# The context between the two latent halves in a layer's value and gate projections

## The chip, the cores and the metric

The kernel runs on one core of a Trainium2 chip. Its time is device microseconds of one execution, as a median over runs. The engines are named as in the profile: PE is TensorE's matmul, PEld its weight load, DVE VectorE, ACT ScalarE, POOL GpSimd, SP SyncE, which issues most transfers.

## What is computed

A two-layer diffusion backbone over 1024 latent tokens (a grid of 16 rows of 64) with a prefix of 256 context tokens; the model is 1024 wide, all of it in float32. The first (even) layer is attention, global and windowed. The change lies in the second (odd) layer, which is the last, so only the latent tokens leave it:

```python
def odd_mixer(h_lat, h_ctx, w_in, w_out, dw_w, dw_b, ln_g, ln_b, rpb, update_ctx):
    cv, cgl, cg, dq, dk, dv, dg = split_cols(h_lat @ w_in, ODD_WIDTHS)
    x_cv, x_cgl, x_cg, x_dq, x_dk, x_dv, x_dg = split_cols(h_ctx @ w_in, ODD_WIDTHS)
    c_dk, c_dv = heads(x_dk, D_HEADS), heads(x_dv, D_HEADS)
    oc = conformer_conv(cv, cgl, cg, dw_w, dw_b, ln_g, ln_b)
    ...
    def d_row(args):
        ...
        kk = jnp.concatenate([c_dk, kr], axis=1)
        vv = jnp.concatenate([c_dv, vr], axis=1)
        return gqa_attend(qr[:, :, :, None, :], kk, vv, bias).reshape(bsz, GRID_W, D_W)
    ...
    y_lat = jnp.concatenate([oc, od * jax.nn.silu(dg)], axis=-1) @ w_out
```

Each of 8 heads of 64 attends from a grid row to the context and to the 8 grid rows around it, with a bias table. Keys and values are projected from latent and context tokens, queries and the gate dg from the latent tokens alone.

## The kernel before

**Precision.** A float32 product is made of three matmuls on a high and a low part of each operand (`mm3`, lines 320 to 322): hi x hi, hi x lo, lo x hi. A high part is a cast on ACT (L298), a low part a subtraction on POOL or DVE (L301). One projection of 128 output rows has a depth of 1024, eight blocks of 128, so 24 matmuls.

**Tokens.** They are kept transposed in three chunks: c = 0 is the context (256 columns), c = 1 and c = 2 are the latent halves (512 each); their high and low parts are called hc for the context and hh, hl for the halves. An accumulation fills one bank of PSUM, called p for these projections.

**Head pairs.** `d_proj(i)` projects pair i of heads (i = 0 to 3), in two parts. First come queries and keys with one set of weights. Then `load_w` brings the weights of value and gate (256 columns, eight blocks, from DRAM into wr, cast into wh on ACT and wl on POOL; there are eight places for wh and wl, so a block of the next set waits until the last projection that reads its place is through). Then a loop over the chunks in the order `VORD`, line 1207:

- the value projection of the chunk. For the context it is copied into vc (ACT, L1212); for a half the columns that its two windows need are copied into vT (ACT, L1217, two copies);
- for a half, the gate projection, its tanh on ACT (L1222) and two products on DVE into sgd (L1224), and the transfer GD to DRAM (L1225);
- transposes of the value in blocks of 128 (trv, PE, L1232): 2 for the context, 4 for half 1, 4 and 2 for half 2; their high and low parts into spv (ACT L298, DVE L301), and the transfer VD to DRAM (L1244).

The tiles sgd and vc, and later xs, a piece of the residual stream that ACT loads (L1411), share two buffers.

**Where the pairs run.** Pair 0 runs under the convolution (whose work is on DVE, POOL and ACT), pair 1 under the layer norm of its result, both with PE to themselves. Pairs 2 and 3 are woven between the steps of the second layer's attention. A group of that attention is one head and one half: it loads keys for a new head (KAt, L363), queries (QH, L1307 and L1308, three buffers; QL, L1309), values (Vt, L1334), bias tables (bm, L1311; bs, L1320) and the gate (gt, L1326) from DRAM, makes row maxima (mx, L1348 and L1356), scores (st, L467 and L471), and the sums over values (ov, L411 to L413), and stores y as O1d (L1379). The output projection (po, by `mm3` too) follows inside the same stretch; oc is the convolution's result as its operand.

**What sets the order.** The program is written as generators that are advanced in turns with fixed numbers (pumps for pairs 0 and 1, weights in a weave for pairs 2 and 3), and a scheduler then puts the instructions of each engine in an order by priority and expected readiness. Each engine works through its queue in that order. The order in `VORD` therefore shifts rows on all five engines.

Of the kernel before, what the change touches and what calls it, by code (L numbers as in the profile page):

```python
# [36 lines left out]
BSW, BMW = 1664, 1080  # L37
CWB = 12
VSH = 5
VORD = (1, 2, 0)  # L40
WBN = 8
TRV = "pp"
HALF = {'half': 3, 'hf': 2}
# [46 lines left out]
def tile_kernel(ctx: ExitStack, tc: tile.TileContext, a, out):  # L90
# [823 lines left out]
    def pair(name, n=512, tag="pair"):  # L914
        return (stg[0] if tag == "spo" else lp).tile([P, 2, NR * NW], F32R, tag=tag, name=nm(name), bufs=STG[tag])[:, :, :n]
# [189 lines left out]
    with ExitStack():  # L1105
# [67 lines left out]
        def d_proj(i):  # L1173
# [32 lines left out]
            vT = pair("vT", 640, "vT").bitcast(F32)  # L1206
            for c in VORD:
                t0, n = CHUNKS[c]
# [431 lines left out]
```

## Time and profile before

| | us |
|---|---|
| median of 3 runs | 1560.27 |
| lowest and highest | 1560.08, 1562.05 |
| profiled execution | 1561.07 |
| its span in the trace | 1559.3 |
| PE busy | 1453.3 (93% of the span) |
| mean granted clock of PE | 0.966 |

The span is the time from the first to the last record of the profiled execution; the rest of its time, 1.8 us, lies around it. A row of a timeline gives the start and the duration in us, engine, line, operation, output and inputs with their tiles, shape and count, and in brackets how long the engine was idle before it and what ended that. In the stage table each stretch has its length, then the busy time of each engine with the number of instructions, the granted clock of PE, the mean busy share of the 16 DMA engines, and GB/s. In the list of waits the numbers are the total, the times, and the longest. Busy time of PE is modelled from pipelined matmuls: a matmul of 512 columns lasts some 0.39 us, and the next starts 0.23 us after it.

### The profile page before, as it was taken

Reading aid. Unit: us, or ns where it says so; the run is one execution under the profiler, and the core shown is the slowest. Engines: PE = TensorE matmul, PEld = TensorE weight load, DVE = VectorE, ACT = ScalarE, POOL = GpSimd, SP = SyncE. Lnnn points to the kernel's source line nnn. Section 1 sums busy time; section 2 is a strip of 40 time slices with the busy share of each in tenths; the row PEclk is TensorE's granted clock in tenths of the full one; section 3 lists DMA queues with packets and bytes.
Section 4 is the critical chain, followed back from the end, with each engine's and each line's share of the span. In section 5 each row is a group of like instructions: output and inputs, shape, how many; then the busy total and the mean of one; then the engine's idle time right before and its main releaser. Section 6 shows DMA issues by size and latency. Waiting matters only on the chain.

```text
span 1559.3 us, 22034 instructions
## 1 busy us (share of the span) xinstructions
PE 1453.3 (93%) x6984; PEld 1174.9 (75%) x6984; DVE 1124.3 (72%) x2172; ACT 763.1 (49%) x1545; POOL 828.7 (53%) x762
## 2 busy tenths in 40 slices
PE   6989999998999999899999889999999998799995
PEld 1888977886888678588887668888787787687785
DVE  4898896788867677555478776999746456587676
ACT  2721354544453755555545655443333455555573
POOL 1561463555455776655646765664542333455575
PEclk9899999999999999999999999999999999899996
DMA  9548245423441135711111121213456888788722
GB/s 337 194 144 263 84 129 175 137 68 117 150 131 46 44 102 167 227 56 53 44 51 62 44 94 53 83 57 127 150 176 220 273 224 251 225 265 239 205 92 108
DMA packets 185613, 221.01 MB, mean 142 GB/s; under 512 B 17420, under 2 KB 139480, under 8 KB 185496
## 3 DMA queue, kind: packets, MB, share of 16 engines
q1 hardware_dynamic: 178832, 208.03, 43.3%
q10 hardware_dynamic: 6664, 11.57, 2.3%
q8 instruction: 55, 0.90, 0.2%
q14 instruction: 62, 0.51, 0.1%
HBM read 159.51 MB, written 60.03 MB: 141 GB/s over the span
## 4 chain that ended last, share of the span: by engine, by line
PE 66%; DVE 13%; DMA 10%; issue 4%; POOL 3%; ACT 2%; SPq 2%; ACTq 0%; DVEq 0%; POOLq 0%
PE p L322 6%; PE p L320 6%; PE p L321 6%; PE ov L411 4%; PE ov L413 4%; PE ov L412 4%; PE po L320 4%; PE po L321 4%; PE po L322 4%; PE st L471 3%; PE st L467 3%; DMA QH<-QD 3%; PE pq L322 2%; PE pq L321 2%; PE pq L320 2%
## 5 line engine op out<-in xcount | busy, mean ns | idle before, releaser
L301 POOL TENSOR_TENSOR pl<-pf,ph 128x512 fp32r<-128x512 f32 (+4 forms) x321 | 394.6, 1240 | 303.7 <-ACT ph L298 244.8
L301 POOL TENSOR_TENSOR wl<-wr,wh 128x256 fp32r<-128x256 f32 (+2 forms) x256 | 198.5, 790 | 214.1 <-ACT wh L298 181.8
L479 ACT ACTIVATE pf<-st 128x512 f32<-128x512 f32 x284 | 167.4, 596 | 185.3 <-PE st L471 140.4
L298 ACT CAST ph<-pf 128x512 fp32r<-128x512 f32 (+4 forms) x364 | 210.8, 588 | 30.9 <-PE ov L412 22.7
L298 ACT CAST wh<-wr 128x256 fp32r<-128x256 f32 (+2 forms) x264 | 103.3, 404 | 171.6 <-DMA wr<-in_od_d_dram 42.8
L320 PE MATMUL p<-hh,wh 128*128 128x512 f32 x448 | 177.9, 399 | 3.2 <-DVE spk L301 1.4
L321 PE MATMUL p<-hl,wh 128*128 128x512 f32 x448 | 178.0, 398 | 0.2 <-POOL hl L301 0.2
L322 PE MATMUL p<-hh,wl 128*128 128x512 f32 x448 | 175.5, 399 | 0.2
L467 PE MATMUL st<-QH,KAt 128*128 128x512 f32 (+4 forms) x364 | 143.3, 395 | 12.5 <-ACT pf L479 10.2
L413 PE MATMUL ov<-pl,Vt 128*128 128x512 f32 (+4 forms) x364 | 144.0, 396 | 6.4 <-POOL pl L301 6.4
L411 PE MATMUL ov<-ph,Vt 128*128 128x512 f32 (+4 forms) x364 | 142.3, 391 | 7.5 <-DVE y L633 3.5
L471 PE MATMUL st<-QL,KBt 68*128 68x512 f32 (+4 forms) x364 | 137.5, 387 | 5.7 <-DVE QL L390 5.6
L412 PE MATMUL ov<-ph,Vt 128*64 128x512 f32 (+4 forms) x364 | 140.5, 386 | 0.0
L1122 DVE SCALAR_TENSOR_TENSOR cps<-U,taps,cps 128x512 f32<-128x512 f32 x184 | 124.4, 749 | 0.0
L591 DVE TENSOR_REDUCE mp<-mx 128x1 f32<-128x512 f32 x128 | 85.7, 682 | 42.7 <-PE mx L590 41.9
L221 DVE SCALAR_TENSOR_TENSOR macc<-mw,csil,macc 128x512 f32<-128x512 f32 x107 | 95.3, 909 | 13.4 <-DMA mw<-in_mod_w_dram 12.3
L320 PEld LDWEIGHTS p<-hh,wh 128*128 128x128 f32 x448 | 84.7, 189 | 23.5 <-DVE spk L301 1.6
L321 PEld LDWEIGHTS p<-hl,wh 128*128 128x128 f32 x448 | 84.7, 189 | 20.8 <-POOL hl L301 0.6
L322 PEld LDWEIGHTS p<-hh,wl 128*128 128x128 f32 x448 | 84.7, 189 | 20.5 <-POOL wl L301 1.0
L467 PEld LDWEIGHTS st<-QH,KAt 128*128 128x128 f32 x364 | 69.7, 192 | 34.9 <-ACT pf L479 19.1
L413 PEld LDWEIGHTS ov<-pl,Vt 128*128 128x128 f32 x364 | 70.5, 194 | 33.8 <-POOL pl L301 12.7
L411 PEld LDWEIGHTS ov<-ph,Vt 128*128 128x128 f32 x364 | 70.6, 194 | 23.2 <-ACT ph L298 5.3
(277 smaller groups left out, 3531.1 us busy)
## 6 DMA issues: line engine op xcount, KB each, us to landing
mw<-in_mod_w_dram SPq DMA_DIRECT2D x34, 512.0 KB, 5.7
bs<-in_d_bs_dram SPq DMA_DIRECT2D x16, 832.0 KB, 7.6
Q<-qs SPq DMA_DIRECT2D x40, 256.0 KB, 2.7
QH<-Q SPq DMA_DIRECT2D x80, 128.0 KB, 2.7
bm<-in_d_bm_dram SPq DMA_DIRECT2D x16, 540.0 KB, 6.2
wr<-in_od_d_dram SPq DMA_DIRECT2D x64, 128.0 KB, 2.8
mw<-in_mod_w_dram SPq DMA_DIRECT2D x28, 256.0 KB, 3.2
wr<-in_ev_qkv_dram SPq DMA_DIRECT2D x32, 192.0 KB, 3.7
```

The lines of the kernel that those rows point to most:

```text
L298: SC.copy(hi, src)
L301: (GP if leng == "g" else VE).tensor_tensor(lo, src, hi.bitcast(F32), op=ALU.subtract)
L320: PE.matmul(o, lh, rh, start=first, stop=False)
L321: PE.matmul(o, lh, rl, start=False, stop=False)
L322: done[0] = PE.matmul(o, ll, rh, start=False, stop=last)
L411: PE.matmul(o, V[:, 64:192], ph[:, :n], start=(t == 0), stop=False)
L412: PE.matmul(g.ov[0:64, q0 : q0 + n], V[:, 0:64], ph[:, :n], start=False, stop=False)
L413: pvs.append(PE.matmul(o, V[:, 64:192], pl[:, :n], start=False, stop=(last and g.sink is None)))
L467: sts.append(PE.matmul(st[:, :n], KA[:, cs], g.QH[:, q0 : q0 + n], start=True, stop=False))
L471: PE.matmul(st[:, :n], KB[0:68, cs], g.QL[0:68, q0 : q0 + n], start=False, stop=True)
L479: SC.activation(pf[:, :n], st[:, :n], AF.Exp, scale=1.0 if g.bias else SCALE)
L1122: VE.scalar_tensor_tensor(pc, uc, w, pc, op0=ALU.mult, op1=ALU.add)
```

## The change

```diff
-VORD = (1, 2, 0)
+VORD = (1, 0, 2)
```

`VORD` is read only in line 1207, so the value projection of the context, its copy and its transposes come between half 1 and half 2 for each head pair. The loop over keys has its own order and is unchanged. The number of instructions of each kind stays the same. From head pair 0's value projection on the order of all engines differs; three places matter below. Names in the rows are tiles with a running number.

First, PE in head pair 0, at the end of the stretch in which three projections are taken in turns as their weights arrive (p_2893 value and p_2896 gate of half 1, then the third). Before:

```order
L320 MATMUL p_2896_11611<-hh_9770,wh_11569 128x512
L321 MATMUL p_2896_11611<-hl_9771,wh_11569 128x512
L320 MATMUL p_2900_11659<-hh_10086,wh_11569 128x512
L321 MATMUL p_2900_11659<-hl_10087,wh_11569 128x512
L322 MATMUL p_2893_11574<-hh_9770,wl_11570 128x512
L322 MATMUL p_2896_11611<-hh_9770,wl_11570 128x512
L322 MATMUL p_2900_11659<-hh_10086,wl_11570 128x512
L1232 MATMUL trv_11649<-ident,vT_11573 128x128 x4
L320 MATMUL p_2903_11696<-hh_10086,wh_11527 128x512
L321 MATMUL p_2903_11696<-hl_10087,wh_11527 128x512
```

Now:

```order
L320 MATMUL p_2896_11611<-hh_9770,wh_11569 128x512
L321 MATMUL p_2896_11611<-hl_9771,wh_11569 128x512
L320 MATMUL p_2900_11659<-hc_10119,wh_11569 128x256
L321 MATMUL p_2900_11659<-hc_10119,wh_11569 128x256
L322 MATMUL p_2893_11574<-hh_9770,wl_11570 128x512
L322 MATMUL p_2896_11611<-hh_9770,wl_11570 128x512
L322 MATMUL p_2900_11659<-hc_10119,wl_11570 128x256
L1232 MATMUL trv_11649<-ident,vT_11573 128x128 x4
L1232 MATMUL trv_11700<-ident,vc_11693 128x128 x2
L320 MATMUL p_2906_11707<-hh_10086,wh_11527 128x512
```

The third projection is the context's, with 256 columns in the same places, and the context's transposes stand at once behind those of half 1.

Second, PE in head pair 3, from the transposes of half 1 (trv_14168) on; mx are the maxima that use newly loaded queries. Before:

```order
L1232 MATMUL trv_14168<-ident,vT_14007 128x128 x4
L413 MATMUL ov_13304<-pl_13405,Vt_12386 128x512
L1348 MATMUL mx_3374_13590<-KAt_12382,QH_13421 128x256 x2
L1356 MATMUL mx_3375_13606<-KAt_12382,QH_13421 128x440
L389 MATMUL trn_13437<-ident,nmt_13410 4x128
L467 MATMUL st_13554<-QH_12995,KAt_12379 128x512
```

Now:

```order
L1232 MATMUL trv_14168<-ident,vT_14007 128x128 x4
L413 MATMUL ov_13301<-pl_13384,Vt_12386 128x512
...
L467 MATMUL st_13554<-QH_12995,KAt_12379 128x512
L471 MATMUL st_13554<-QL_12996,KBt_12380 128x512
L320 MATMUL p_3522_14178<-hc_10119,wh_13961 128x256
L321 MATMUL p_3522_14178<-hc_10119,wh_13961 128x256
...
L320 MATMUL p_3522_14178<-hc_10119,wh_13991 128x256
L321 MATMUL p_3522_14178<-hc_10119,wh_13991 128x256
L1348 MATMUL mx_3374_13590<-KAt_12382,QH_13400 128x256 x2
L1356 MATMUL mx_3375_13606<-KAt_12382,QH_13400 128x440
```

The maxima moved behind 17 of the 24 matmuls of the context's projection (and a pair of scores); the same head's queries are in a tile of another number.

Third, SP at the end of head pair 3, with the keys (KAt) and queries (QH) of the next head, the output projection's weights (wr) and the last values of the pair (VD). Before:

```order
L1379 DMA O1d<-y_3413_13771 64x512
L1244 DMA VD_7433<-spv_14454 128x512
L1320 DMA bs_13908<-in_d_bs_dram 128x1664
L363 DMA KAt_12379<-KD_7428 64x1536 x2
L1307 DMA QH_13914<-QD_7424 64x512
L1308 DMA QH_13914<-QD_7424 64x512
L1309 DMA QL_13915<-QD_7424 64x512
L1334 DMA Vt_12386<-VD_7431 128x2x128
L1334 DMA Vt_12386<-VD_7431 128x5x128
L331 DMA wr_14794<-in_od_wo_dram 128x256
```

Now:

```order
L331 DMA wr_15082<-in_od_wo_dram 128x256
L1225 DMA GD_7437<-sgd_14360 256x1x256
L1244 DMA VD_7433<-spv_14446 128x768
L1244 DMA VD_7433<-spv_14446 128x256
L1244 DMA VD_7433<-spv_14454 128x512
L363 DMA KAt_12379<-KD_7428 64x1536
L1320 DMA bs_13908<-in_d_bs_dram 128x1664
L363 DMA KAt_12379<-KD_7428 64x1536
L1307 DMA QH_13914<-QD_7424 64x512
L1308 DMA QH_13914<-QD_7424 64x512
```

The gate and all values of half 2 are now the last transfers ahead of the keys, the table bs stands between the two loads of keys, and the weight loads wr_14794 to wr_15082 come before all of them, where they came behind the queries.

## The prediction

> **What bounds the kernel now.** I read first the page's busy times and its chain of work that ended last.
>
> ```profile
> PE 1453.3 (93%) x6984; PEld 1174.9 (75%) x6984; DVE 1124.3 (72%) x2172; ACT 763.1 (49%) x1545; POOL 828.7 (53%) x762
> PE 66%; DVE 13%; DMA 10%; issue 4%; POOL 3%; ACT 2%; SPq 2%; ACTq 0%; DVEq 0%; POOLq 0%
> ```
>
> TensorE is busy 93% of the span and carries most of the chain, and the change gives it the same matmuls in another order. It can therefore only change how long TensorE idles and at what clock it runs. The table by stage says where there is any idle time to win or lose.
>
> ```profile
> core 0: us, PE busy (x) PEld busy (x) DVE busy (x) ACT busy (x) POOL busy (x), PEclk, DMA share, GB/s
> 1090.00:1112.00 22.00, 21.80 (x104) 17.11 (x103) 20.29 (x34) 10.98 (x22) 17.61 (x13) 1.00 0.37 115
> 1144.00:1178.00 34.00, 33.44 (x177) 27.69 (x175) 21.29 (x38) 16.33 (x37) 13.30 (x14) 1.00 0.44 145
> 1178.00:1215.00 37.00, 35.34 (x170) 28.96 (x171) 17.53 (x36) 12.31 (x28) 11.77 (x15) 1.00 0.70 223
> 1300.00:1345.00 45.00, 39.62 (x198) 32.23 (x197) 31.06 (x72) 23.89 (x53) 14.48 (x17) 0.92 0.77 235
> 1345.00:1365.00 20.00, 13.18 (x50) 9.28 (x49) 9.58 (x21) 12.02 (x26) 10.77 (x12) 0.74 0.90 239
> ```
>
> The first two stretches are the projections of head pairs 0 and 1 (under the convolution and under the layer norm): full, so they can only lose. The last two are the fourth pair's value and gate projections, woven into the attention of the second layer, and the attention just behind: 12.2 us idle, and a clock below 1. What the waits there are for:
>
> ```profile
> PE mx L1348 <- DMA QH<-QD: 8.4, 4, 4.0
> PE trv L1232 <- ACT vc L1212: 1.4, 1, 1.4
> PE p L320 <- DVE r L423: 0.8, 1, 0.8
> ```
>
> They are loads of the queries (QH), the copy of the context's values (vc), and one bank. The first of the two big stalls, in order of time on TensorE:
>
> ```profile
> 1311.84 0.47 PE L1348 MATMUL mx<-KAt,QH 128*128 128x256 f32 x2 [2.81 <-DMA QH<-QD]
> 1315.57 0.77 PE L320 MATMUL p<-hh,wh 128*128 128x512 f32 x1 [0.77 <-DVE r L423]
> 1316.13 0.63 PE L321 MATMUL p<-hl,wh 128*128 128x512 f32 x1
> ...
> 1320.52 0.40 PE L320 MATMUL p<-hh,wh 128*128 128x512 f32 x1
> 1320.75 0.39 PE L321 MATMUL p<-hl,wh 128*128 128x512 f32 x1
> ```
>
> After 2.81 and 0.77 us of idling the matmuls last 0.63 instead of 0.39 us and start 0.43 apart instead of 0.23: half clock until 1320.3. The second stall, on TensorE and in the chain:
>
> ```profile
> 1356.06 0.41 PE L471 MATMUL st<-QL,KBt 68*128 68x224 f32 x1
> 1360.47 0.76 PE L1348 MATMUL mx<-KAt,QH 128*128 128x256 f32 x2 [4.00 <-DMA QH<-QD]
> ...
> 1364.67 0.40 PE L413 MATMUL ov<-pl,Vt 128*128 128x512 f32 x1
> ```
>
> ```profile
> 1342.99 0.20 ACT vc L1212
> ...
> 1343.76 5.88 DMA xs<-X
> ...
> 1349.66 0.56 SPq L363
> ...
> 1350.27 0.86 SPq L1307
> ...
> 1351.18 9.05 DMA QH<-QD
> ```
>
> The keys' second load (L363) was let go when a transfer of xs landed at 1349.64; the queries are issued behind it on SP and take 9.05 us.
>
> **The change, part by part.** No instruction is added or removed. Of the 24 matmuls of a projection, those of the context have 256 columns. First and last of one such set:
>
> ```profile
> 1172.22 0.36 PE L320 MATMUL p<-hc,wh 128*128 128x256 f32 x1
> ...
> 1175.06 0.28 PE L322 MATMUL p<-hc,wl 128*128 128x256 f32 x1
> ```
>
> So the context projection takes 24 x 0.12 = 2.9 us, and one of a latent half (0.2335 from start to start above) 5.6 us.
>
> *1. Head pair 0, while its weights arrive.* Three projections share the weights as they come in; the third is now the context's, 2.7 us shorter. The pace is set by the weights' low parts:
>
> ```profile
> 1101.94 2.14 POOL L301 TENSOR_TENSOR wl<-wr,wh 128x256 fp32r<-128x256 f32 x3
> 1106.39 0.75 POOL L301 TENSOR_TENSOR wl<-wr,wh 128x256 fp32r<-128x256 f32 x1
> ```
>
> ```profile
> 1102.74 0.50 PE L322 MATMUL p<-hh,wl 128*128 128x512 f32 x1
> 1109.15 0.86 PE L322 MATMUL p<-hh,wl 128*128 128x512 f32 x3
> 1110.06 0.77 PE L1232 MATMUL trv<-ident,vT 128*128 128x128 f32 x4
> ```
>
> In before TensorE just missed waiting at 1102.7 (0.1 us) and had 2 us in hand when the last low part was done (1107.14). With 2.7 us less to do it stands again until 1102.7 and ends about 1.1 us earlier instead of 2.7. The 2.7 us are not saved, they come back as work later: a loss of **1.6** (bounds 0, if POOL runs ahead, and 2.7, if nothing is hidden).
>
> *2. The context's transposes.* In before they stood 11 to 18 matmuls behind the context projection; for pairs 0, 1 and 2 they now stand right behind the first half's transposes, 0.5 to 0.6 us after the projection. ACT must by then have made:
>
> ```profile
> 1109.59 0.75 ACT L1217 COPY vT<-p 128x320 f32<-128x320 f32 x2 [1.96 <-PE p L322]
> 1110.22 0.62 ACT L1222 ACTIVATE sgd<-p 128x512 f32<-128x512 f32 x1
> ...
> 1120.91 0.36 ACT L1212 COPY vc<-p 128x256 f32<-128x256 f32 x1
> ```
>
> ```profile
> 1110.87 0.75 DVE L1224 SCALAR_TENSOR_TENSOR sgd<-sgd,p 128x256 f32<-128x256 f32 x2
> ```
>
> With the copies at 1109.6 to 1110.3 and the tanh until 1110.8, vc is there at 1111.1, and the transposes would be due at 1110.6: 0.5. Behind them the next projection waits for a bank that the gate holds until DVE's two products (0.75) are through: up to 1.1 in all; I take **0.8**. In pair 1 DVE has the layer norm's operations queued ahead of these products; nearest row is the same, so again **0.8** (bounds 0 and 3, four such pairs of operations ahead). Pair 2: **0.3**. Part of the lateness ends in waits on DVE that TensorE already has after 1178:
>
> ```profile
> PE p L320 <- DVE spk L301: 1.4, 1, 1.4
> PE p L320 <- DVE spv L301: 0.8, 1, 0.8
> ```
>
> I credit **-1.0** of these 2.2. So the attention begins 2.5 us later (bounds 0 and 6).
>
> *3. First stall (pair 3).* 17 of the 24 context matmuls, 2.0 us, now stand between the transposes and the maxima that wait for QH; the 2.81 falls by 2.0. Behind the maxima TensorE now meets the context's own transposes, with vc queued on ACT among the casts of the convolution's output: I charge 1.0 (bounds 0 and 2). The half clock cost (1320.3 - 1315.6)/2 = 2.3 us; with the idling cut to under 2 us I count 1.6 of it as gained, an estimate between 0 and 2.3. Sum **-2.6**.
>
> *4. End of pair 3.* The 1.4 us wait for vc goes, as vc is no longer last: **-1.4**. What is late next is the gate's tanh and products, and its GD and VD transfers.
>
> *5. Second stall.* The order of SP shows the output projection's weight loads (wr) issued before the keys now, not around the queries, and the keys no longer wait for xs: QH waits for a transfer of long before. In their place GD and three VD stand directly ahead. If the projection ends at the same time as before (about 1342.5, since vc is being copied in the chain's row at 1342.99), the tanh (0.6), the products (0.8), transposes and split bring VD to about 1345.5 and QH to 1347.8 instead of 1350.27: **-2.4**. Bounds: -7 if the whole wait and its half clock go, +4 if DVE is late (below). The wr moved ahead load the same 16 DMA engines, so QH's 9.05 us need not shrink; I leave it.
>
> The Trainium skill's "DMA: Bandwidth & Descriptors", section "Issuing engines are not separate DMA queues", says that transfers issued by different engines run on the same engines and interleave. The trace agrees (share 0.90 while xs from ACT and QH from SP are both under way). By it the four wr moved ahead could cost QH what they gain in place; the -2.4 would become -1 or so, an estimate.
>
> *6. The next queries.*
>
> ```profile
> 1369.76 0.40 PE L322 MATMUL po<-oc,wl 128*128 128x512 f32 x1
> 1370.79 0.47 PE L1348 MATMUL mx<-KAt,QH 128*128 128x256 f32 x2 [0.64 <-DMA QH<-QD]
> ```
>
> These maxima now stand ahead of the six output matmuls (6 x 0.24) that ended at 1370.0, so the wait grows from 0.64 to about 2.1: **+1.4** (bounds 0 and 2.4). From SP's row 833 on both orders are the same, and I count nothing after.
>
> Sum: 1.6 + 1.9 - 1.0 - 2.6 - 1.4 - 2.4 + 1.4 = -2.5 us. The profiled execution took 1561.07 us (span 1559.3 and 1.8 around it), 0.8 above the median 1560.27. 1561.07 - 2.5 - 0.8 = **1557.8 us**.
>
> **Rivals.** *Slower.* The second half's gate is now last, and its GD and VD stand ahead of keys and queries on SP. DVE was nearly full there:
>
> ```profile
> 1340.00:1345.00 5.00, 3.61 (x23) 2.94 (x22) 4.36 (x14) 2.23 (x7) 3.03 (x5) 1.00 0.88 239
> ```
>
> If the softmax's operations keep the products and the split back so that VD issues after 1347.4 (1349.66 less 2.2 us, four issues of 0.56 like that of L363, for GD and VD), QH is later than before. With VD 4 us behind that point the stall is 8 instead of 4: term 5 turns from -2.4 to +4, the sum to +3.9, the time to 1564.2; with the upper bound of 1 and most of that of 2 it reaches 1567. For it: DVE's 4.36 of 5. Against it: fewer transfers are left to issue between VD and QH. *Much faster.* Short idling costs no clock, so both stalls lose their half clock: besides the terms above, the rest of stall two (1.6), its slow stretch (4.2/2 = 2.1) and the rest of stall one's (0.7) go, 4.4 more: 1553.4. Against it: the first stall's longest wait was 2.81 us and half clock followed. The Trainium skill's "TensorE: Matmul & The Clock Gate", section "Why this matters for your kernels", has this rule: no idle gaps above about 3 us, or the clock halves. By it what is left of both stalls would be free of that cost; this trace does not agree on the size, since a gap of 2.81 was enough. *Nothing:* the loads decide when TensorE goes on, and each gain is waited away: 1560.3.
>
> **How the numbers follow.** Forecast 0.40 (its own range 1555 to 1561), slower 0.33, much faster 0.24, nothing 0.03. 0.2% is 3.1 us, about what a measurement of this kernel can tell from no change: faster means under 1557.15, slower over 1563.4. Faster: 0.24 and 0.16 of the forecast's 0.40, whose middle lies close to that line. Same: 0.22 of the forecast and 0.03. Slower: 0.33 and 0.02. The range runs from 1551.5 (much faster with term 2 at its lower bound) to 1567.
>
> **What would show it.** Right: TensorE idle 0.5 to 2 us in pair 0 before 1112; the vc wait after 1340 gone; the QH waits near 1311 under 1 us and near 1358 under 2.5 us, with QH issued before 1348 by the clock of before; a wait of 2 us at the next maxima. Wrong: an idle stretch over 3 us in pair 1, VD issued after 1347.4, or half clock longer than before.

## The result: 0.55% slower, and the profile after

The changed kernel took 1567.75 us (median of 14 runs, 1563.13 to 1574.64), the kernel before beside it on the same chips 1560.42 us (14 runs, 1554.28 to 1564.68). The ratio is 1.0055 with a 95% interval of 1.0037 to 1.0073, so the change costs about 8.6 us (5.8 to 11.4; the two medians alone differ by 7.3). The forecast was 1557.8, and the median lies 0.75 us above the upper end of the range.

The profiled execution after took 1570.84 us (span 1569.1, mean granted clock 0.964), 9.8 us more span than before. Busy times and chain of the page, to be held against those of before:

```profile
PE 1459.5 (93%) x6984; PEld 1177.9 (75%) x6984; DVE 1128.5 (72%) x2172; ACT 765.0 (49%) x1545; POOL 827.6 (53%) x762
PE 69%; DVE 13%; DMA 8%; issue 3%; POOL 3%; ACT 2%; SPq 1%; ACTq 0%; POOLq 0%; DVEq 0%
```

The matmuls are as many as before, and the difference is idling and slow clock again. The table by stage, in the five stretches of before:

```profile
core 0: us, PE busy (x) PEld busy (x) DVE busy (x) ACT busy (x) POOL busy (x), PEclk, DMA share, GB/s
1090.00:1112.00 22.00, 20.77 (x109) 16.91 (x108) 20.20 (x34) 10.11 (x18) 18.07 (x14) 1.00 0.49 159
1144.00:1178.00 34.00, 32.13 (x164) 26.71 (x163) 20.14 (x34) 13.12 (x29) 11.66 (x12) 0.95 0.43 141
1178.00:1215.00 37.00, 37.00 (x182) 30.32 (x181) 23.00 (x41) 15.37 (x34) 11.23 (x13) 1.00 0.59 195
1300.00:1345.00 45.00, 41.06 (x210) 34.08 (x209) 31.33 (x69) 26.64 (x58) 19.70 (x23) 0.96 0.84 257
1345.00:1365.00 20.00, 14.98 (x62) 10.11 (x61) 14.47 (x37) 13.01 (x26) 9.62 (x10) 0.86 0.91 261
```

The projections of pairs 0 and 1, which had next to no idle time (0.2 and 0.6 us), now have some (1.2 us in the first row, 1.9 in the second, where the clock falls to 0.95). The two stretches with the big stalls became fuller and faster: 3.9 instead of 5.4 us idle at clock 0.96 instead of 0.92, and 5.0 instead of 6.8 us at 0.86 instead of 0.74. By these rows alone the change would seem to give more than it takes (12.1 us idle in all instead of 14.6), though each trace is cut here by its own clock.

To see where the sum is made, I follow the **lost time** of TensorE in both traces: at each row of its timeline the idle time ahead of it, and what the time to the next row's start exceeds full pace (0.2335 us for 512 columns, in proportion for fewer). A wait counts whole at the mark before which it begins. The sum starts from one instruction that both kernels have just ahead of the first changed row, the first query copy of pair 0; it starts at 1073.12 before and at 1076.87 after.

```profile
1073.12 0.60 ACT L1180 ACTIVATE spq<-p 128x512 fp32r<-128x512 f32 x1 [1.79 <-PE p L322]
```
```profile
1076.87 0.60 ACT L1180 ACTIVATE spq<-p 128x512 fp32r<-128x512 f32 x1 [1.81 <-PE p L322]
```

So 3.75 of the 9.8 us arose ahead of anything that the change touches; they belong to that execution and not to the change. The other 6.0, by the clock of before (all times of other kernels are set back so that this row agrees):

| until | lost in before | after, more than before |
|---|---|---|
| 1144 (pair 0) | 1.7 | +2.7 |
| 1178 (pair 1's projections) | 4.6 | +5.1 |
| 1262 (first groups of attention) | 11.9 | +4.9 |
| 1345 (pair 3 done) | 25.0 | +0.9 |
| 1380 | 38.0 | +1.6 |
| 1420 | 39.3 | +4.9 |
| end | 64.3 | +6.0 |

How the short matmuls are counted moves the first column by some 10% and the second by 0.6 at most. The loss of the first part is won back in pair 3, and then the kernel loses a second time where the prediction counted nothing.

### Pair 0 and pair 1

Waits of TensorE from 1085 to 1215, after:

```profile
PE p L320 <- DVE sgd L1224: 2.0, 2, 1.8
PE p L322 <- POOL wl L301: 0.6, 1, 0.6
```

Before there were two others, 1.4 and 0.8 us for DVE, shown in the prediction; both are gone. The first line is two waits, 1.84 and 0.17 us. The 0.6 us for a weight's low part is pair 0's, as forecast. The 1.84 us is pair 1's, on TensorE:

```profile
1169.10 0.44 PE L1232 MATMUL trv<-ident,vc 128*128 128x128 f32 x2
1171.38 0.47 PE L320 MATMUL p<-hh,wh 128*128 128x512 f32 x1 [1.84 <-DVE sgd L1224]
1171.69 0.59 PE L321 MATMUL p<-hl,wh 128*128 128x512 f32 x1
...
1174.63 0.63 PE L322 MATMUL p<-hh,wl 128*128 128x512 f32 x1
1175.06 0.43 PE L320 MATMUL p<-hh,wh 128*128 128x512 f32 x1
```

Nine matmuls from 1171.38 to 1175.06 took 3.68 instead of 2.10 us. With the wait of 1.84 that is 3.4 us. The wait is for the bank that half 1's gate product leaves. DVE's timeline after:

```profile
1164.34 2.74 DVE L1164 SCALAR_TENSOR_TENSOR uc<-uc,lng,s 128x512 f32<-128x512 f32 x4 [4.68 <-ACT s L1159]
1166.99 1.91 DVE L1167 TENSOR_SCALAR uc<-uc,lnb 128x512 f32<-128x512 f32 x2
1168.83 1.75 DVE L1168 SCALAR_TENSOR_TENSOR uc<-thl,uc 128x512 f32<-128x512 f32 x1
1170.50 0.74 DVE L1224 SCALAR_TENSOR_TENSOR sgd<-sgd,p 128x256 f32<-128x256 f32 x2
```

and before:

```profile
1160.02 0.75 DVE L1224 SCALAR_TENSOR_TENSOR sgd<-sgd,p 128x256 f32<-128x256 f32 x2 [2.94 <-ACT sgd L1222]
1161.36 2.74 DVE L1164 SCALAR_TENSOR_TENSOR uc<-uc,lng,s 128x512 f32<-128x512 f32 x4 [0.59 <-ACT s L1159]
```

Before, the two products came first and the layer norm's seven steps (uc) behind them. Now they stand behind those steps, 6.2 us of work, and TensorE meets the bank earlier, as the context's projection in between is 2.7 us shorter than half 2's was.

### Pair 3 and what follows

Waits of TensorE from 1215 to 1500, after, the five longest lines. Before, the first two lines of this view were QH with 9.9 us in six waits and KAt with 3.8 in two.

```profile
PE mx L1348 <- DMA QH<-QD: 4.4, 2, 2.8
PE ov L411 <- ACT vc L1212: 3.8, 1, 3.8
PE mx L1348 <- DMA Vt<-VD: 2.7, 1, 2.7
PE ov L411 <- ACT ph L298: 2.4, 2, 1.6
PE mx L1348 <- DMA KAt<-KD: 2.1, 1, 2.1
```

The waits for queries fell by more than half, and others took their place: casts on ACT, the copy of the context's values, and one of 2.7 us that the view puts down to values (Vt), though these maxima read only keys and queries. The first stall is now this, on TensorE (the maxima at 1318.50 have no wait any more):

```profile
1318.50 0.47 PE L1348 MATMUL mx<-KAt,QH 128*128 128x256 f32 x2
...
1324.32 0.47 PE L411 MATMUL ov<-ph,Vt 128*128 128x512 f32 x1 [3.76 <-ACT vc L1212]
...
1326.41 0.78 PE L320 MATMUL p<-hh,wh 128*128 128x512 f32 x1
```

ACT's timeline shows what ov really waited for:

```profile
1321.60 0.33 ACTq L1402 DMA_DIRECT2D oc<-Oc  x1
1321.97 0.62 ACT L298 CAST oc<-oc 128x512 fp32r<-128x512 f32 x1 [2.33 <-DMA oc<-Oc]
...
1323.57 0.48 ACT L298 CAST ph<-pf 128x352 fp32r<-128x352 f32 x1
1323.96 0.36 ACT L1212 COPY vc<-p 128x256 f32<-128x256 f32 x1
```

ACT stood 2.33 us for a piece of the convolution's output (oc), whose cast is ahead of ph and vc in its queue; TensorE needed both. The prediction named this queue and charged 1.0 us for it.

For the second stall, the chain of work that ended last, after:

```profile
1351.94 5.63 DMA KAt<-KD
...
1358.97 0.42 ACT pf L477
...
1360.28 0.77 PE ov L411
...
1366.63 6.00 DMA QH<-QD
...
1372.78 0.48 PE mx L1348 x2
```

Before, TensorE waited 4.00 us for queries at 1360.47. Now TensorE waits four times for ACT and DVE between 1348.5 and 1360.3 (1.61, 0.76, 0.87, 1.11 us). The last of them has the keys ahead of it: the cast that copies the keys' high part into KBt (L557) waits 1.32 us on ACT for KAt, and an exponential's scaling pf stands behind that cast. The first has a weight ahead of it: ACT stood 1.96 us until 1346.04 for a piece wr of the output projection, whose cast is ahead of ph. Then it waits 2.82 us for the next queries at 1372.78.

### The profile page after: what moved, and what is told of

Same layout as the page of the kernel before. It is cut to its first block, busy times and chain, and to the rows that moved or that the text cites. A ratio compares the mean times of both kernels' runs of the same rounds, so it can differ in the third digit from the quotient of the medians.

```text
span 1569.1 us, 22043 instructions
## 1 busy us (share of the span) xinstructions
PE 1459.5 (93%) x6984; PEld 1177.9 (75%) x6984; DVE 1128.5 (72%) x2172; ACT 765.0 (49%) x1545; POOL 827.6 (53%) x762
## 4 chain that ended last, share of the span: by engine, by line
PE 69%; DVE 13%; DMA 8%; issue 3%; POOL 3%; ACT 2%; SPq 1%; ACTq 0%; POOLq 0%; DVEq 0%
PE p L321 6%; PE p L322 6%; PE p L320 6%; PE ov L411 4%; PE ov L413 4%; PE ov L412 4%; PE st L471 4%; PE st L467 4%; PE po L320 4%; PE po L321 4%; PE po L322 4%; PE pq L322 2%; PE pq L321 2%; PE pq L320 2%; DMA mw<-in_mod_w_dram 2%
## 5 line engine op out<-in xcount | busy, mean ns | idle before, releaser
L298 ACT CAST wh<-wr 128x256 fp32r<-128x256 f32 (+2 forms) x264 | 103.0, 404 | 166.5 <-DMA wr<-in_ev_qkv_dram 39.3
L322 PEld LDWEIGHTS p<-hh,wl 128*128 128x128 f32 x448 | 84.6, 189 | 20.4 <-POOL wl L301 1.4
```

The source lines that it names most:

```text
L298: SC.copy(hi, src)
L322: done[0] = PE.matmul(o, ll, rh, start=False, stop=last)
```

## The experiments

Four theories. **A**: the loss is made in pair 1, where the gate's products stand behind the layer norm on DVE. **B**: it is made in pair 3, where ACT stands for oc. **C**: it has no single place. Changing the order of the context redraws the queues of all five engines, and each later wait for a load, a cast or a bank is drawn anew; any other small change of the order would cost about as much. **D**: having the context second costs by itself, in whatever pair. Later came **E**: ACT standing at the KBt cast for the keys.

### One pair at a time

The order of chunks is given for each pair, and only one pair has the new one. For pair 0:

```diff
-VORD = (1, 2, 0)
+VORD = ((1, 0, 2), (1, 2, 0), (1, 2, 0), (1, 2, 0))
-            for c in VORD:
+            for c in VORD[i]:
```

and so on with (1, 0, 2) at the second, third and fourth place. What was expected, pair 0:

> Only head pair 0 takes the context second. Theory A (the loss is made under the layer norm, in pair 1, by the bank that the gate's products hold): 0 to +2 us against before, with TensorE waits of 0.6 (wl), 0.3 (vc) and 0.2 (sgd) us near 1107 to 1115. Theory B (the loss is made in pair 3 by ACT's queue): the same 0 to +2. Theory C (no single place; any other order rolls the later waits anew): anywhere from -4 to +6, with changed waits behind 1215.

Pair 1:

> Only head pair 1 takes the context second. Theory A: +3 to +5 us, with one wait of TensorE of 1.5 to 2 us on sgd and half clock for some 4 us behind it, both before 1180. Theory B: within 1 us of before. Theory C: anywhere from -4 to +6 with the sum not explained by the waits before 1215.

Pair 2:

> Only head pair 2 takes the context second. Theory A: 0 to +1 us. Theory B: 0 to +1 us. Theory C: -4 to +6.

Pair 3:

> Only head pair 3 takes the context second. Theory A: -3 to 0 us, since the waits of pair 3 that go and come about cancel. Theory B: +4 to +8 us, with a TensorE wait of 3 us or more on ACT's copies and casts (vc, ph) behind the casts of oc. Theory C: -4 to +6.

Measured, beside 1560.04 of the kernel before (20 runs): pair 0 alone 1569.15 (ratio 1.0058, 1.0033 to 1.0082), pair 1 alone 1574.64 (1.0091, 1.0070 to 1.0111), pair 2 alone 1559.64 (1.0000, 0.9984 to 1.0016), pair 3 alone 1569.57 (1.0056, 1.0035 to 1.0076). The four sum to about +32 us, and the change with all four costs 8.6. They don't add. Every range on record was missed for pairs 0, 1 and 3, that of theory C (-4 to +6) too; its range in the later expectations, +3 to +14, was set after these results.

Where each loses lies elsewhere than the edit. Two waits of pair 0 alone, one of pair 1 alone and two of pair 3 alone:

```profile
1183.10 0.77 PE L320 MATMUL p<-hh,wh 128*128 128x512 f32 x1 [3.64 <-DVE spv L301]
...
1310.62 0.77 PE L1348 MATMUL mx<-KAt,QH 128*128 128x256 f32 x2 [4.68 <-DMA QH<-QD]
```
```profile
1233.37 0.74 PE L1356 MATMUL mx<-KAt,QH 128*128 128x440 f32 x1 [4.43 <-DVE mp L1357]
```
```profile
1373.66 0.55 PE L1348 MATMUL mx<-KAt,QH 128*128 128x256 f32 x1 [4.29 <-DMA QH<-QD]
...
1464.00 0.47 PE L1348 MATMUL mx<-KAt,QH 128*128 128x256 f32 x2 [4.51 <-issue]
```

With pair 1 alone changed, the stall of the theory A is not there at all: TensorE has no wait for sgd up to 1215, and its lost time at 1178 is not above that of before (the row below stands at a mark that a wait of before, 0.8 us, straddles). The loss begins some 60 us later in attention, and more than half of it comes after 1420. With pair 3 alone changed, TensorE's work runs like before's as far as 1345 (-0.2 us), and the loss comes at 1373 and at 1464 (by the clock of its own rows), where the work is attention and output projection. The lost time of all these, more than before, by the clock of before (one profiled execution each):

| until | pair 0 | pair 1 | pair 2 | pair 3 |
|---|---|---|---|---|
| 1178 | 5.1 | -1.6 | -0.4 | -0.5 |
| 1262 | 20.4 | 4.9 | 0.6 | 0.4 |
| 1345 | 17.6 | 3.7 | 0.7 | -0.2 |
| 1380 | 6.4 | 5.9 | 0.1 | 3.4 |
| 1420 | 8.3 | 7.0 | 2.5 | 3.2 |
| end | 12.5 | 15.2 | 1.3 | 10.4 |

Pair 0 alone is 20.4 us behind at 1262 and has 14.0 of them back at 1380: before itself loses 26.1 us between these two points, 9.5 of them idle in five waits for queries, and in pair 0 alone TensorE has no wait at all from 1312 to 1380. So a kernel that comes late to a stretch that waits for loads can get most of its loss back there. A falls as the place of the loss, and D does not hold either, with pair 2 at nothing.

### Taking the two new stalls away

From the changed kernel. First (A), the layer norm's scaling of half 1 is held until pair 1's products of half 1 are through:

```diff
-            yield
+            while [(yield)] and (1, 1) not in sgi: pass
...
-                VE.scalar_tensor_tensor(uc[:, i], uc[:, i], lng[:, i : i + 1], s2, op0=ALU.mult, op1=ALU.mult)
+                with (tc.issue_after(sgi[1, 1].ins) if c == 0 else ExitStack()):
+                    VE.scalar_tensor_tensor(uc[:, i], uc[:, i], lng[:, i : i + 1], s2, op0=ALU.mult, op1=ALU.mult)
...
-                        VE.scalar_tensor_tensor(sgh[:, h_], sgh[:, h_], 1.0, halves(pp)[:, h_], op0=ALU.add, op1=ALU.mult)
+                        sgi[i, c] = VE.scalar_tensor_tensor(sgh[:, h_], sgh[:, h_], 1.0, halves(pp)[:, h_], op0=ALU.add, op1=ALU.mult)
```

> The changed kernel, with the layer norm's scaling of its first half held until the gate's products of half 1 in pair 1 are issued, so that DVE has these products first. Theory A: the 1.84 us wait on sgd and the half clock behind it go, 3 to 4 us faster than the changed kernel, so +3 to +5 against before. Theory B: within 1 us of the changed kernel (+7). Theory C: -4 to +8 against before.

Second (B), the loads and casts of oc are held until pair 3's copy vc:

```diff
-                    SC.copy(vc[:, :n], pp[:, :n])
+                    vci[i] = SC.copy(vc[:, :n], pp[:, :n])
...
-        run(out1_alloc())
+        with tc.issue_after(vci[3].ins): run(out1_alloc())
```

> The changed kernel, with the loads and casts of oc held behind pair 3's copy vc, so that ACT does not stand waiting for oc's transfers ahead of the casts that TensorE needs. Theory B: the 3.76 us wait and 1.7 us of half clock behind it go, 4 to 6 us faster than the changed kernel, +1 to +3 against before. Theory A: that wait goes too, but what is gained is given back at later waits for queries, so at most 2 us faster, +5 to +7 against before.

Third, both edits together:

> The changed kernel with both: gate's products first in pair 1, and oc's loads and casts behind vc in pair 3. Theory A and B together: 7 to 10 us faster than the changed kernel, so from -3 to +1 against before. Theory A alone: +2 to +4. Theory C: no relation to the two single edits.

Measured beside 1559.36 of before: the first 1585.26 (1.0165, 1.0132 to 1.0198), the second 1570.74 (1.0069, 1.0043 to 1.0095), both 1581.82 (1.0144, 1.0116 to 1.0172). Each stall went: the lost time at 1178 fell from 5.1 to 0.8 us over before with the first, that at 1320 from 0.3 to -3.0 with the second. Nothing of it reached the end, and no range on record was met. New waits of the first and of the second:

```profile
1295.30 0.80 PE L1348 MATMUL mx<-KAt,QH 128*128 128x256 f32 x2 [3.30 <-DMA QH<-QD]
...
1473.36 0.77 PE L1348 MATMUL mx<-KAt,QH 128*128 128x256 f32 x2 [4.24 <-issue]
```
```profile
1368.61 0.47 PE L1348 MATMUL mx<-KAt,QH 128*128 128x256 f32 x2 [2.65 <-DMA QH<-QD]
...
1455.82 0.74 PE L1348 MATMUL mx<-KAt,QH 128*128 128x256 f32 x2 [5.17 <-issue]
```

So both stalls were read rightly, and taking them away gains nothing at the end. Each of these edits is itself a new order, so a small gain could be hidden in them. The first also holds the layer norm itself up, so how much of its 17 us over the changed kernel is that and how much is new order stays open. B is not borne out as the cause of the total.

### The keys' second copy without ACT (E)

KBt holds a second copy of the keys' high part, for the product with the queries' low part. In the second layer it is brought by a third load instead of a cast on ACT, with the same values, in the changed kernel and in that of before:

```diff
-            SY.dma_start(KA[s_ * 64 : (s_ + 1) * 64, :].bitcast(F32), ks[:, s_])
+            SY.dma_start(KA[s_ * 64 : (s_ + 1) * 64, :].bitcast(F32), ks[:, s_]); s_ and layer[0] and SY.dma_start(KB[0:64, :].bitcast(F32), ks[:, 0])
...
-        SC.copy(KB[0:64, :], KA[0:64, :].bitcast(F32))
+        if not layer[0]: SC.copy(KB[0:64, :], KA[0:64, :].bitcast(F32))
```

In the changed kernel:

> The changed kernel, with the copy of the keys' high part (KBt, second layer) made by a transfer instead of ACT's cast, so that ACT never stands in its queue waiting for keys to land. Theory E (much of the later loss is ACT standing at that cast in front of the softmax's casts): 4 to 10 us faster than the changed kernel, -3 to +4 against before. Theory C: another draw, +3 to +14 against before.

In the kernel before:

> The kernel before with the same edit. Theory E: 2 to 8 us faster than before, since ACT waits 24.7 us at that cast there too. Theory C: another draw, +3 to +14.

Measured beside 1562.64: 1574.30 (1.0066, 1.0046 to 1.0087) and 1573.72 (1.0064, 1.0037 to 1.0091). E is not borne out: taking the cast away gained nothing in the one, and it cost the other as much as the change does. The edit also adds a transfer for each head, so that cost may be the transfer's and not the new order's. The two orders of chunks are now equal.

### Redrawing the order without the change (C)

The sharpest test of C leaves the context last and moves the weave by one step: `WV[0]` and `WV[1]` say how many steps of attention are spread over pair 2's and pair 3's projections. Four kernels in the old order of chunks, and the same four in the new:

```diff
-WV = (73, 53, 77, 24, 12)
+WV = (74, 53, 77, 24, 12)
```

and likewise 72 for 73, and 54 or 52 for 53. Expected, in the old order, 74, 54, 52 and 72:

> The kernel before, old order of chunks, with pair 2's projections woven over 74 instead of 73 steps of the attention: the same work, other queue orders from pair 2 on. Theory C (any other order rolls the later waits anew, and the order of before is a favourable draw): slower than before by 3 to 14 us, as p0, p1 and p3 were. Rival D (the context in second place is itself what costs): within 3 us of before.

> The kernel before, with pair 3's projections woven over 54 instead of 53 steps. Theory C: slower than before by 3 to 14 us. Rival D: within 3 us of before.

> Old order of chunks, pair 3 woven over 52 steps. If leaving the queue order of before is what costs (Theory C): +3 to +14 us against before, like w54 and w74. If not: within 3 us.

> Old order of chunks, pair 2 woven over 72 steps. Theory C: +3 to +14 us against before. If leaving the queue order of before costs nothing: within 3 us.

In the new order, 74, 54, 52 and 72:

> New order of chunks, pair 2 woven over 74 steps. Theory C: +3 to +14 us. Theory A: 5 us or more above w74 (so +13 or more).

> New order of chunks, pair 3 woven over 54 steps. Theory C: in the range of the kernels with the old order, +3 to +14 us. Theory A: 5 us or more above w54 (so +13 or more).

> New order of chunks, pair 3 woven over 52 steps. If the new order costs nothing of its own (Theory C): +3 to +14 us against before, in the same range as w52 and w54. If it costs some 5 us of its own for the solo stage (Theory A): 5 us or more above w52.

> New order of chunks, pair 2 woven over 72 steps. Theory C: +3 to +14 us against before. Theory A: 5 us or more above w72.

Measured, as ratios to the kernel before beside it:

| WV | old order | new order |
|---|---|---|
| 74 | 1.0054 (1.0030 to 1.0077) | 1.0046 (1.0029 to 1.0063) |
| 54 | 1.0050 (1.0027 to 1.0073) | 1.0045 (1.0025 to 1.0066) |
| 52 | 1.0049 (1.0027 to 1.0071) | 1.0030 (1.0004 to 1.0056) |
| 72 | 1.0016 (0.9995 to 1.0037) | 1.0054 (1.0032 to 1.0075) |
| mean | 1.0042 | 1.0044 |
| 73, 53 (as given) | 1 | 1.0055 |

The traces show that these are fewer kernels than they seem. On PE, DVE, POOL and SP, 74 runs the same sequence of instructions as 54, and 72 the same as 52, in either order of chunks; on ACT at most four records stand in another place. So there are two other orders of the weave, each measured twice. 72 and 52 in the old order, 1.0016 and 1.0049, are one kernel on two chips: two measurements can lie 0.3% apart, a little more than their intervals allow. Taken together:

| weave | old order | new order |
|---|---|---|
| 74 and 54 | 1.0052 | 1.0046 |
| 72 and 52 | 1.0033 | 1.0042 |
| as given | 1 | 1.0055 |

An order of the weave that has nothing to do with the context costs 0.33 to 0.52%, up to as much as the whole change. With either of these two the context's new place makes no difference that can be told (-0.0007 and +0.0009, each known to about 0.002, some 3 us), so a cost or a gain of its own of that size can't be excluded. That 72 lies 5.9 us higher in the new order than in the old, which was the sign of theory A, is within this spread. The step is not quite neutral either: it moves one step of attention against all that is woven behind it.

These profiles also say where the loss lies. By the clock of before, neither group of five below differs among itself ahead of 1364 us in anything but those records of ACT; what a step in the weave redraws stands behind. The lost time of TensorE (here the time gone by since the common row, less the full pace of the columns done), one profile each, lowest and highest:

| until | 1180 | 1262 | 1345 | 1364 | from 1364 to the end |
|---|---|---|---|---|---|
| old order, as given | 5.6 | 14.1 | 27.7 | 39.1 | 30.1 |
| old order, other four | 5.3 to 6.0 | 14.6 to 15.4 | 26.2 to 29.0 | 37.4 to 39.9 | 33.3 to 43.0 |
| new order, as given | 10.9 | 19.2 | 28.5 | 37.6 | 37.4 |
| new order, other four | 9.8 to 10.3 | 18.4 to 19.3 | 26.7 to 28.7 | 37.8 to 39.3 | 36.5 to 38.9 |

The 4 to 5 us that the context's new place costs in pairs 0 and 1 are there in all five profiles, and in none are they left at 1345 or at 1364. What the change costs is lost behind 1364, where the old order as given loses 30.1 us and every other order in this table 33 to 43. Why it loses least there is not shown. One place where 74 (old order) loses more, and the same maxima in before:

```profile
1459.77 0.77 PE L1348 MATMUL mx<-KAt,QH 128*128 128x256 f32 x2 [5.50 <-DMA KAt<-KD]
```
```profile
1453.10 0.69 PE L1348 MATMUL mx<-KAt,QH 128*128 128x256 f32 x2 [2.03 <-DMA KAt<-KD]
```

The keys come in two loads. In 74 they take 10.9 and 11.7 us from issue to landing, in before 5.8 and 11.2; the second load is about as long in both, but in 74 it is issued 6.8 us later by the common clock. The same maxima wait 5.02 us in 54 and 4.51 in pair 3 alone.

A larger wait of 74 is not made by its order:

```profile
1314.74 0.76 PE L1348 MATMUL mx<-KAt,QH 128*128 128x256 f32 x2 [7.00 <-DMA QH<-QD]
```
```profile
1303.19 11.42 DMA QH<-QD
```

Up to there SP and TensorE do the same in the same order as in before, where these maxima waited 2.81 us and this load took 7.8 us. In the six profiles with that order (before, 74, 54, 72, 52 and pair 3 alone) the maxima wait 2.81, 7.00, 2.89, 2.75, 2.10 and 3.50 us; those of the second stall wait 4.00, 1.97, 3.62, 1.01 and 2.32 us in the first five. The size of a wait in one profile is one of a wide spread.

C stands in a narrower form: an order other than the one given loses more behind 1364, whether or not the context is moved. It is not without exception: pair 2 alone costs nothing that can be told (1.0000). None of the 17 kernels, 13 different orders, was clear of before on the faster side.

## Why the prediction was wrong, point by point

**Terms 1 and 2, pair 0: right.** 1.6 + 0.8 were forecast, 2.7 measured at 1144, with waits of 0.6 us for a low part, 0.35 for a high part and 0.17 to 0.33 for vT, vc and a bank.

**Term 2, pair 1: too small.** 0.8 was taken, with 3 as the upper bound; it was 3.4 (1.84 idle and 1.6 of half clock). The mechanism was the named one, layer norm ahead of the products on DVE, but the value was taken from pair 0's row, where DVE is free for the products as soon as the tanh is done (1110.87). The bound left the half clock out.

**The credit of -1.0: about right.** Both waits for DVE (0.8 and 1.4) went, and a new one of 1.06 for a weight's cast came at 1219.59. From 2.7 + 3.4 the attention's first groups are 4.9 us late at 1262, where 2.5 were forecast; the difference is pair 1's.

**Terms 3 and 4: right in sum by luck, other in parts.** -2.6 and -1.4 were forecast; from 1262 to 1345 the lost time falls by 4.0. The 2.81 us wait for QH and the 1.4 for vc at the end went as said; two more QH waits of before (1.07 at 1275.52 and 0.94 at 1293.12) went as well, unforeseen, and paid for the new stall, which was charged at 1.0 with 2 as its bound and came to 3.76 with half clock behind it. That these came out even is luck, and the 2.81 and 4.00 us from which terms 3 and 5 were priced are each one of a wide spread, as shown above. (The 8.4 us of waits for queries in the prediction's list belong to a wider stretch than its table; from 1300 to 1365 there are two, 6.8 us.)

**Terms 5 and 6: wrong by 1.7.** -2.4 and +1.4 were forecast, the stretch 1345 to 1380 shows +0.7. In the clock of before (4.65 us off here: 3.75 and the 0.9 of the table) VD was issued at 1345.3 to 1347.2 and QH at 1349.0, 1.3 us earlier than before instead of 2.4. The wait for these queries went, but four shorter ones on ACT and DVE took its place, behind a weight's cast and the keys' cast among others, which were not among the rivals; the next maxima wait 2.82 us where 2.1 were forecast. The slower rival's condition, VD after 1347.4, was missed by 0.2 us, so it is not what made the kernel slower.

**"I count nothing after": the step that failed.** From 1380 to the end the changed kernel loses 4.4 us more than before, 3.3 of them by 1420. That SP's rows read the same from 833 on was taken to mean that nothing behind term 6 changes. In the traces SP's transfers agree only from 1421.8 us by the clock of before (the last 79 of 977), 51 us behind the maxima of term 6, and TensorE's order differs as far as 1543.8. One place on SP in between, before:

```profile
1392.69 0.45 SPq L1307 DMA_DIRECT2D QH<-QD  x1
1393.19 0.59 SPq L1308 DMA_DIRECT2D QH<-QD  x1
```

and after, with what TensorE then waits for:

```profile
1398.30 0.78 SPq L1307 DMA_DIRECT2D QH<-QD  x1
1399.17 0.55 SPq L1379 DMA_DIRECT2D O1d<-y  x1
1399.77 0.58 SPq L1320 DMA_DIRECT2D bs<-in_d_bs_dram  x1
1400.40 0.56 SPq L1308 DMA_DIRECT2D QH<-QD  x1
...
1408.16 0.47 PE L1348 MATMUL mx<-KAt,QH 128*128 128x256 f32 x2 [1.60 <-DMA QH<-QD]
```

The second load of these queries is issued 2.1 us behind the first instead of 0.5, and TensorE waits 1.60 us where before had no wait; another wait of 1.25 us, for DVE, follows at 1416.77. So the term that was put at nothing is the one that decides: by the ten profiles above the change costs nothing up to 1364 us. With pair 3 alone changed 7.0 of the 10.4 us come after 1380.

Sum: forecast -2.5, in the two profiled executions +6.0. Of the 8.5 between them 2.4 lie in pairs 0 to 2, nothing in 3 and 4, 1.7 in 5 and 6 (no more than profiles of one order differ by), and 4.4 in what was left out. Of the signs that the prediction gave for being right all came but one (QH issued at 1349.0 and not before 1348), and the time still went the other way: the signs were all local. The sum priced each place as if the rest stayed put. The single pairs show that it doesn't (+9, +14, 0 and +9 against +8.6 for all four), and the steps in the weave show that another order of what stands behind 1364 costs some 5 to 8 us though the context stays where it was. A rival "any other order is a little worse" was the one to have, and it was missing; the one called "nothing" had 0.03.

## What to carry to other kernels

In a kernel whose order a scheduler makes over five engines, a gain read from one wait is only good up to the next place that waits for a load; price it by the end, and expect single edits not to add. Take several profiles before you price a wait: those of one order here show 1.0 to 4.0 us for the same one. Before a difference of half a per cent is put down to what a change is meant to do, run a redraw of the order that leaves the change out (one step more in a weave) in both versions, and compare the orders, as two settings can give the same one. Where the redraw alone moves the time as much, the kernel before is a good draw, and what the change was meant to do is not the cause. Where an experiment takes a stall away and the end does not come earlier, the stall alone did not set the time, however big it looks; but such an edit is a new order too and needs the same control.

## What was not expected of the hardware

**What a gap on TensorE costs is a matter of chance.** In the 19 profiles I took every gap of TensorE of 0.9 us or more from 1050 us on that had full clock ahead and no other gap over 0.5 us in the 5 us ahead or the 3.5 us behind, and looked in the records of the granted clock whether half clock began in it or in those 3.5 us: 156 gaps. Half clock came after 11 of the 74 under 1.7 us, after 32 of the 52 from 1.7 to 3.0 us, and after all 30 from 3.0 us up; its median length was 6.8 us in the first and the last group and 3.4 us in the middle one. The row at 1171.38 above is such a case: 1.84 us, then half pace. The row at 1368.61 is the other: 2.65 us, and the clock stayed whole. So a gap that is cut from 4 to 2 us keeps its clock penalty in some of the runs and not in others; the prediction had reckoned with a part of it. The Trainium skill's "TensorE: Matmul & The Clock Gate", section "Why this matters for your kernels", puts the limit at about 3 us; from there up these gaps agree, but 43 of the 126 shorter ones were followed by half clock too.

**The runs of one kernel spread widely.** The kernel before gave 1554.28 to 1564.68 us over 14 executions, 0.67%. Differences like those above need the interval, and a single profile with 6.0 or 13 us more than before is one of such a spread.
